# The first two column pairs of each feed-forward stage by plain block products instead of Winograd products

## The chip, the cores and the metric

The kernel runs on one core of one Trainium2 chip. The metric is the device time of one execution in microseconds (us); before the change it is 2248.64 us, the median of 3 runs (2248.58 to 2249.43).

## What is computed

One layer: a feed-forward stage, a mixer of four branches, a second feed-forward stage, over 1024 tokens with 1024 features, in float32. The change touches the two feed-forward stages alone (D = 1024, F = 2816):

```python
def _rmsnorm(x, w):
    y = x * rsqrt(mean(x * x, axis=-1) + EPS)
    return y * w

def _swiglu(x, wg, wu, wd):
    return (silu(x @ wg) * (x @ wu)) @ wd

x = x + 0.5 * _swiglu(_rmsnorm(x, ffn1_norm), ffn1_wg, ffn1_wu, ffn1_wd)
...
x = x + 0.5 * _swiglu(_rmsnorm(x, ffn2_norm), ffn2_wg, ffn2_wu, ffn2_wd)
```

## The kernel before

**Values.** x is held transposed, as 8 blocks of 128 features by 1024 tokens, in tiles of two blocks and 512 tokens (one half of the tokens). Each float32 operand of a product is split into hi and lo (ScalarE, ACT, writes hi; VectorE, DVE, writes lo, in `split` or `left_plain`), and a product of blocks is three matmuls on TensorE (PE): hi·hi, lo·hi, hi·lo (`one`, L1161 to L1163). All matmuls of the stages are 128x128 weights against 128x512 values.

**Gate and up products.** F is cut into 22 columns f of 128; each has a gate and an up part. `gate_up` computes for each f the two 512-token halves of gate and up with Winograd's seven products instead of eight: the left blocks are A11, A12 (tokens' first half, features' first and second half), A22, and the sums S1 to S4 of blocks of x; the right ones are made from the weights of f in `prep_gate` and `prep_up`. A product is 4 blocks of 128 features, so 12 matmuls, and a column is 84. `first` is A11 times gate, `second` adds A12 times gate to the same PSUM tile, `rest` issues S2, S1, S4, A22 and S3 and adds the products on DVE. `act` multiplies by the norm's factor `scale` and applies SiLU; `spill` sends each two columns' sums to DRAM. `down` then multiplies by wd, likewise by Winograd's scheme.

**The norm.** The gain goes into the left blocks, the factor 1/rms (one number for each token) is applied behind the products, in `act`. `square` and `add_squares` make the sum of squares, `mean` (16 tiny matmuls `ms`, L1099) sums over features, `rsqrt` is a chain of 11 small DVE operations that ends in `rs_y` (L157), 8 matmuls `r` (L1117) spread it over the partitions and ACT copies it to `scale` (L1118).

**The start of a stage.** The sums S1 to S4 need all of x and time on DVE. To give PE work in the meantime, `left` opens columns 0 to 3 ahead: `open` issues `first`, `open_second` issues `second`, so 8 products of 12 matmuls; the sums, their splits and the squares are written between them. Then `gate_up` takes the S2 and S1 products of column 0, and `rms` is a background generator that issues `ms` after them and `r` after a pause. In stage 1, x comes from DRAM, the sums of squares are added on DVE; in stage 2, x comes from the mixer's last product (`product`, L260 to L266) and they are added on GpSimd (POOL).

**What sets the order.** PE follows the program's order; ACT, DVE, POOL and SP (which issues the DMAs) follow an order that the scheduler sets when the program is built, each strictly in that order.

Of the kernel before, what the change touches and what calls it, by code (L numbers as in the profile page):

```python
# [976 lines left out]
class Ffn:  # L977
# [9 lines left out]
    def __init__(self, net, n, es):  # L987
        self.net, self.nc, self.n = net, net.nc, n
        pool = lambda name, bufs: es.enter_context(
            net.tc.tile_pool(name=f"{name}{n}", bufs=bufs, reuse_waits="tile")  # L990
        )
# [4 lines left out]
        self.preps, self.raw_gate = {}, {}
        self.gain = net.col(f"ffn{n}_norm")
        self.ms, self.squares = None, {}
        self.opened = {}

# [203 lines left out]
    def act(self, f, g, u):  # L1204
# [22 lines left out]

    def open(self, f):

        self.prep_gate(f)  # L1230
        self.opened[f] = [*self.first(f), None]

    def open_second(self, f):
        self.opened[f][2] = self.second(f, self.opened[f][0])
        if f:
            self.raw_gate.pop(f)

    def gate_up(self, also):

        net = self.net  # L1240
        self.acts = {}
        waiting = []

        def acts():
            net.bg.finish()
            while waiting:
                waiting.pop(0)()

        for f in range(NF):
            self.prep_up(f)  # L1250
            self.prep_gate(f + 1)
            if f in self.opened:
                _, t, g = self.opened.pop(f)
                waiting.append(self.rest(f, t, g, mid=acts))
            else:
                x, t = self.first(f)
                waiting.append(self.rest(f, t, None, x))
            if f:
                acts()
            if f == 2:  # L1260
                also()
# [160 lines left out]
def build(ctx, tc, a, cols):  # L1422
# [15 lines left out]
    def left(ffn, x0, x1, engine, late):  # L1438

        ffn.open(1)  # L1440
        for i in range(2):
            ffn.open_second(i)
        ffn.open(2)
        ffn.left_s2(x0[:2], x1[2:])
        ffn.prep_up(0)
        ffn.open(3)
        for i in (2, 3):
            ffn.open_second(i)
        ffn.left_s1(x1[:2], x1[2:])
        ffn.add_squares(engine)  # L1450
        for q, kp in late:
            ffn.square((x0, x1)[q][kp], q, kp)
            ffn.add_squares(engine)
        ffn.left_rest(x0[:2], x0[2:], x1[2:])
        n.bg.add(ffn.rms(4, 7))

    with ExitStack() as es:
# [20 lines left out]
        for q, xs in ((0, x0), (1, x1)):
            for kp in range(2):
                ffn.square(xs[kp], q, kp)  # L1480
        ffn.left_cross(x0[:2], x1[:2])
        left(ffn, x0, x1, nc.vector, [(q, kp) for q in range(2) for kp in (2, 3)])
# [117 lines left out]
```

## Time and profile before

| | us |
|---|---|
| median of 3 runs | 2248.64 |
| the profiled execution | 2247.78 |
| its span | 2246.0 |
| PE busy | 2191.7 (98%) |
| DVE busy | 1377.5 (61%) |
| ACT busy | 873.0 (39%) |
| chain that ended last: PE | 89% |
| chain that ended last: DVE | 6% |

The profiled execution is one run; its span is from the first to the last instruction, and 1.78 us of its time lie around it. The chain that ended last is followed back from the last instruction: it says which engine the end waited for. PE is busy nearly all the time over the whole span, so a share of the span says little about the start of a stage; what a step there costs is read in the stretch itself.

### The profile page before, as it was taken

How to read it: one execution, taken by the hardware profiler on the slowest of the kernel's cores; microseconds unless marked ns; L12 is line 12 of the kernel's file. 1: busy time of each engine (PE TensorE's matmuls, PEld its weight loads, DVE VectorE, ACT ScalarE, POOL GpSimd, SP SyncE). 2: the span in 40 equal slices, each digit the busy share in tenths (PEclk: the TensorE clock that was granted, in tenths of full speed). 3: DMA queues.
4: the chain of work that ended last, by engine and by line, in shares of the span. 5: the costliest groups of instructions: out<-in, count | busy, mean ns of one | idle time of the engine just before them, and what ended most of it. 6: DMA issues, size and time to landing. Idle time of an engine off the chain costs nothing.

```text
span 2246.0 us, 26117 instructions
## 1 busy us (share of the span) xinstructions
PE 2191.7 (98%) x10144; PEld 1782.3 (79%) x10144; DVE 1377.5 (61%) x1925; ACT 873.0 (39%) x1154; POOL 327.3 (15%) x227
## 2 busy tenths in 40 slices
PE   6899999999999999999999999999889999999999
PEld 5688888888887777788877778888678888888887
DVE  8788787887773446315255233035778777778764
ACT  7223332234443533326477363134423323224332
POOL 0000000000013344322343434411000000000000
PEclk9899999999999999999999999999989999999999
DMA  4233232394333122231111222116223232249432
GB/s 153 82 100 113 91 117 94 129 330 164 105 130 110 52 75 72 82 118 56 59 55 45 81 80 78 53 52 195 67 94 117 94 111 101 98 144 326 150 118 94
DMA packets 115484, 246.15 MB, mean 110 GB/s; under 512 B 11296, under 2 KB 23200, under 8 KB 115360
## 3 DMA queue, kind: packets, MB, share of 16 engines
q1 hardware_dynamic: 115360, 244.48, 32.5%
q8 instruction: 79, 1.29, 0.2%
q14 instruction: 45, 0.37, 0.1%
HBM read 182.05 MB, written 62.39 MB: 109 GB/s over the span
## 4 chain that ended last, share of the span: by engine, by line
PE 89%; DVE 6%; ACT 2%; issue 2%; POOL 1%; DMA 0%; SPq 0%; POOLq 0%; ACTq 0%; DVEq 0%
PE X L1163 3%; PE X L1161 3%; PE X L1162 3%; PE S2p L1163 2%; PE S2p L1161 2%; PE S2p L1162 2%; PE S4p L1161 2%; PE Ad L1345 2%; PE S4p L1163 2%; PE S1p L1161 2%; PE S4p L1162 2%; PE Ad L1344 2%; PE S1p L1162 2%; PE S1p L1163 2%; PE Ad L1343 2%; PE S3p L1161 2%
## 5 line engine op out<-in xcount | busy, mean ns | idle before, releaser
L56 POOL TENSOR_TENSOR wlo<-raw,whi 128x1024 fp32r<-128x1024 f32 x56 | 136.0, 2429 | 249.3 <-ACT whi L55 237.6
L1011 ACT ACTIVATE uhi<-gu 128x1024 fp32r<-128x1024 f32 x44 | 46.8, 1063 | 263.5 <-issue 135.8
L55 ACT ACTIVATE whi<-raw 128x1024 fp32r<-128x1024 f32 x72 | 76.0, 1057 | 184.6 <-PE o L261 22.3
L964 DVE TENSOR_TENSOR gt<-gt,wb 128x512 f32<-128x512 f32 x48 | 32.9, 686 | 135.7 <-PE wb L956 77.5
L1011 ACT ACTIVATE ghi<-gu 128x1024 fp32r<-128x1024 f32 x44 | 46.7, 1061 | 168.0 <-DMA gu<-wgu 154.8
L191 POOL TENSOR_TENSOR nm0lo<-res,nm0hi 128x1024 fp32r<-128x1024 f32 x2 | 5.0, 2484 | 638.2 <-ACT nm0hi L190 638.2
L1011 ACT ACTIVATE ahiS<-inS 128x1024 fp32r<-128x1024 f32 (+1 forms) x48 | 46.9, 989 | 131.3 <-PE Dd L1344 31.7
L1012 DVE TENSOR_TENSOR aloS<-inS,ahiS 128x1024 fp32r<-128x1024 f32 (+1 forms) x48 | 54.5, 1135 | 60.9 <-ACT ahiS L1011 60.9
L1161 PE MATMUL X<-A11hi,ghi 128*128 128x512 f32 x176 | 71.9, 409 | 13.2 <-ACT ghi L1011 13.2
L1208 ACT ACTIVATE a<-a 128x1024 f32<-128x1024 f32 x44 | 46.8, 1063 | 85.6 <-DVE a L1207 85.6
L965 POOL TENSOR_TENSOR m<-m,gt 128x512 f32<-128x512 f32 x48 | 62.2, 1297 | 119.8 <-DVE gt L964 118.1
L1163 PE MATMUL X<-A11hi,glo 128*128 128x512 f32 x176 | 72.4, 412 | 5.5 <-DVE glo L1012 5.5
L1163 PE MATMUL S2p<-S2hi,tlo 128*128 128x512 f32 x176 | 70.6, 401 | 4.0 <-DVE tlo L1012 4.0
L1161 PE MATMUL S2p<-S2hi,thi 128*128 128x512 f32 x176 | 70.2, 399 | 3.8 <-ACT thi L1011 3.8
L1162 PE MATMUL X<-A11lo,ghi 128*128 128x512 f32 x176 | 71.2, 404 | 0.0
L1161 PE MATMUL X<-A12hi,ghi 128*128 128x512 f32 x176 | 68.6, 390 | 2.6 <-ACT t L1171 2.6
L1162 PE MATMUL S2p<-S2lo,thi 128*128 128x512 f32 x176 | 70.1, 399 | 0.0
L1161 PE MATMUL S4p<-S4hi,uhi 128*128 128x512 f32 x176 | 69.4, 394 | 0.0
L1162 PE MATMUL S4p<-S4lo,uhi 128*128 128x512 f32 x176 | 68.7, 391 | 0.0
L1163 PE MATMUL S4p<-S4hi,ulo 128*128 128x512 f32 x176 | 68.7, 390 | 0.0
L1345 PE MATMUL Ad<-ahiA,dloA 128*128 128x512 f32 x176 | 68.7, 390 | 0.0
L1161 PE MATMUL S1p<-S1hi,thi 128*128 128x512 f32 x176 | 68.7, 390 | 0.0
(1209 smaller groups left out, 6774.2 us busy)
## 6 DMA issues: line engine op xcount, KB each, us to landing
gu<-wgu SPq DMA_DIRECT2D x94, 512.0 KB, 3.5
raw<-w_in SPq DMA_DIRECT2D x56, 512.0 KB, 3.5
acts<-s SPq DMA_DIRECT2D x88, 256.0 KB, 2.9
wd<-wd SPq DMA_DIRECT2D x40, 512.0 KB, 6.5
inS<-acts SPq DMA_DIRECT2D x40, 512.0 KB, 3.7
acts<-a SPq DMA_DIRECT2D x66, 256.0 KB, 3.3
inA<-acts SPq DMA_DIRECT2D x30, 512.0 KB, 3.6
res<-x SPq DMA_DIRECT2D x16, 512.0 KB, 6.8
```

The source lines that it names most:

```text
L55: nc.scalar.activation(hi, raw, AF.Copy)
L56: getattr(nc, self.lo_engine[i]).tensor_tensor(lo, raw, hi.bitcast(F32), op=ALU.subtract)
L965: nc.gpsimd.tensor_tensor(m, m, g, op=ALU.add)
L1011: self.nc.scalar.activation(hi, src, AF.Copy)
L1012: self.nc.vector.tensor_tensor(lo, src, hi.bitcast(F32), op=ALU.subtract)
L1161: mm(ps, whi[:, s], hi, start=start and k == 0, stop=False, skip_group_check=True)
L1162: mm(ps, whi[:, s], lo, start=False, stop=False, skip_group_check=True)
L1163: mm(ps, wlo[:, s], hi, start=False, stop=k == 3, skip_group_check=True)
L1208: nc.scalar.activation(g, g, AF.Silu)
L1343: mm(outs[t], whi[:, j, m], ahi[:, j], start=first, stop=False, skip_group_check=True)
L1344: mm(outs[t], whi[:, j, m], alo[:, j], start=False, stop=False, skip_group_check=True)
L1345: mm(outs[t], wlo[:, j, m], ahi[:, j], start=False, stop=last, skip_group_check=True)
```

## The change

In both stages columns 0 and 1 are no longer made by Winograd's seven products, and no column is opened ahead. Instead they are made by eight plain block products: for each f, each half of the tokens q and each of gate and up (j), `half` issues 8 blocks of 128 features, 24 matmuls (L1246 to L1248), into one PSUM tile, and ACT copies it to `early` (L1250). That needs the left blocks A11, A12, A21 and A22 split as they are (A21 is new) and the weights of columns 0 and 1 split as they are (`plain_right`). `early_act` applies scale and SiLU to both columns at the start of `gate_up`, which then takes columns 2 to 21 by the seven products as before. `rms` is no generator any more: `ms` is issued behind the plain products of column 0, `r` (`spread`) behind those of column 1. Each column now ends with its own `act`. The diff, cut:

```diff
-    def left_rest(self, a11, a12, a22):
+    def left_rest(self, a11, a12):
         for kp in range(2):
             self.scaled_with(a12[kp], a12[kp], 4 + 2 * kp, self.s2[kp], ALU.subtract)
         self.left_split("S4", a12)
-        self.left_plain("A22", a22, 4)
         self.left_split("S3", a11)
...
+    def plain_right(self, f, j):
+        tag = "rg" if f == 0 else ("rt", "ru")[j]
+        raw = self.load(2 * f + j)
+        self.plain[f, j] = self.split(raw, *(self.t4(tag, f"p{part}{f}{j}", F32R) for part in ("hi", "lo")))
+
+    def half(self, f, q):
+        mm = self.nc.tensor.matmul
+        names = (("A11", "A12"), ("A21", "A22"))[q]
+        for j in range(2):
+            whi, wlo = self.plain[f, j]
+            ps = self.net.ps(f"h{f}{q}{j}")
+            for k in range(NK):
+                s = slice(k % 4 * P, (k % 4 + 1) * P)
+                hi, lo = (t[:, k % 2] for t in self.xc[names[k // 4]][k % 4 // 2])
+                mm(ps, whi[:, k // 4, s], hi, start=k == 0, stop=False, skip_group_check=True)
+                mm(ps, whi[:, k // 4, s], lo, start=False, stop=False, skip_group_check=True)
+                mm(ps, wlo[:, k // 4, s], hi, start=False, stop=k == NK - 1, skip_group_check=True)
+            self.early[f, q, j] = t = self.t2("ts"[q], f"e{f}{q}{j}")
+            self.nc.scalar.copy(t, ps)
+
+    def early_act(self, f):
+        nc = self.nc
+        V = nc.vector
+        a = self.t4("a", f"a{f}")
+        for q in range(2):
+            g, u = (self.early[f, q, j] for j in range(2))
+            V.tensor_tensor(g, g, self.scale[:, q], op=ALU.mult)
+            nc.scalar.activation(g, g, AF.Silu)
+            V.tensor_tensor(u, u, self.scale[:, q], op=ALU.mult)
+            V.tensor_tensor(a[:, q], g, u, op=ALU.mult)
+        self.put(f, a)
...
-        for f in range(NF):
+        for f in range(2):
+            self.early_act(f)
+        for f in range(2, NF):
             self.prep_up(f)
             self.prep_gate(f + 1)
...
     def left(ffn, x0, x1, engine, late):
-        ffn.open(1)
-        for i in range(2):
-            ffn.open_second(i)
-        ffn.open(2)
-        ffn.left_s2(x0[:2], x1[2:])
-        ffn.prep_up(0)
-        ffn.open(3)
-        for i in (2, 3):
-            ffn.open_second(i)
-        ffn.left_s1(x1[:2], x1[2:])
-        ffn.add_squares(engine)
-        for q, kp in late:
+        for j in range(2):
+            ffn.plain_right(1, j)
+        ffn.half(0, 0)
+        for q, kp in late[:4]:
             ffn.square((x0, x1)[q][kp], q, kp)
             ffn.add_squares(engine)
-        ffn.left_rest(x0[:2], x0[2:], x1[2:])
-        n.bg.add(ffn.rms(4, 7))
+        ffn.left_plain("A21", x1[:2], 0)
+        ffn.left_plain("A22", x1[2:], 4)
+        ffn.half(1, 0)
+        for q, kp in late[4:]:
+            ffn.square((x0, x1)[q][kp], q, kp)
+            ffn.add_squares(engine)
+        ffn.half(0, 1)
+        ffn.rms()
+        ffn.left_cross(x0[:2], x1[:2])
+        ffn.left_s2(x0[:2], x1[2:])
+        ffn.half(1, 1)
+        ffn.prep_gate(2)
+        ffn.prep_up(2)
+        ffn.spread()
+        ffn.left_s1(x1[:2], x1[2:])
+        ffn.left_rest(x0[:2], x0[2:])
```

Three places, as the engines' orders show them. ACT at the start of stage 1, before the change (t is the copy of `first`'s PSUM tile X, ghi the hi part of a column's gate weights, sq a square):

```order
L1171 COPY t0_1_149<-X0_136 128x512
L1011 ACTIVATE ghi1_1_157<-gu2_1_155 128x1024
L1080 ACTIVATE sq00_1_183<-n0x0_1_114 128x1024
L1080 ACTIVATE sq01_1_185<-n0x1_1_122 128x1024
L1080 ACTIVATE sq10_1_187<-n1x0_1_175 128x1024
```

and the same place after it (e is the copy of a plain product's PSUM tile h, phi the hi part of a plain column's weights):

```order
L1079 ACTIVATE sq00_1_234<-n0x0_1_114 128x1024
L1079 ACTIVATE sq01_1_236<-n0x1_1_122 128x1024
L1079 ACTIVATE sq02_1_239<-n0x2_1_136 128x1024
L1079 ACTIVATE sq03_1_242<-n0x3_1_138 128x1024
L1250 COPY e001_1_232<-h001_207 128x512
L1029 ACTIVATE A21hi1_1_247<-n1x1_1_162,c_small_76 128x512
L1011 ACTIVATE phi10_1_170<-gu2_1_168 128x1024
```

The split of the third set of weights, phi10, now stands behind the copy of the second plain product h001 and one half of A21.

DVE at the end of the norm's chain in stage 1, before the change (tlo is the lo part of column 1's weights for S2 and S1):

```order
L1147 TENSOR_TENSOR tt1_1_528<-gu3_1_525,tt1_1_528 128x512
L155 TENSOR_TENSOR f1rs_t_454<-f1rs_y_453 128x8
L1150 TENSOR_TENSOR gu2_1_523<-gu2_1_523,tt1_1_528 128x512
L156 SCALAR_TENSOR_TENSOR f1rs_t_454<-f1rs_t_454,v1_451 128x8
L157 SCALAR_TENSOR_TENSOR f1rs_y_453<-f1rs_t_454,f1rs_y_453 128x8
L155 TENSOR_TENSOR f1rs_t_454<-f1rs_y_453 128x8
L1012 TENSOR_TENSOR tlo1_1_532<-tt1_1_528,thi1_1_531 128x1024
L156 SCALAR_TENSOR_TENSOR f1rs_t_454<-f1rs_t_454,v1_451 128x8
L157 SCALAR_TENSOR_TENSOR f1rs_y_453<-f1rs_t_454,f1rs_y_453 128x8
L155 TENSOR_TENSOR f1rs_t_454<-f1rs_y_453 128x8
L156 SCALAR_TENSOR_TENSOR f1rs_t_454<-f1rs_t_454,v1_451 128x8
L157 SCALAR_TENSOR_TENSOR f1rs_y_453<-f1rs_t_454,f1rs_y_453 128x8
```

and after it (S1lo and S3lo are lo parts of left sums, gu7 the up weights of column 3):

```order
L1012 TENSOR_TENSOR glo3_1_604<-gu6_1_601,ghi3_1_603 128x1024
L155 TENSOR_TENSOR f1rs_t_408<-f1rs_y_407 128x8
L1012 TENSOR_TENSOR tlo2_1_507<-tt2_1_503,thi2_1_506 128x1024
L156 SCALAR_TENSOR_TENSOR f1rs_t_408<-f1rs_t_408,v1_405 128x8
L1012 TENSOR_TENSOR S1lo0_1_541<-n1x0_1_160,S1hi0_1_540 128x1024
L157 SCALAR_TENSOR_TENSOR f1rs_y_407<-f1rs_t_408,f1rs_y_407 128x8
L1012 TENSOR_TENSOR S1lo1_1_543<-n1x1_1_162,S1hi1_1_542 128x1024
L155 TENSOR_TENSOR f1rs_t_408<-f1rs_y_407 128x8
L1144 TENSOR_TENSOR gu7_1_713<-gu7_1_713 128x512
L156 SCALAR_TENSOR_TENSOR f1rs_t_408<-f1rs_t_408,v1_405 128x8
L1012 TENSOR_TENSOR S3lo1_1_563<-n0x1_1_122,S3hi1_1_562 128x1024
L157 SCALAR_TENSOR_TENSOR f1rs_y_407<-f1rs_t_408,f1rs_y_407 128x8
```

Between v, which reads `ms`, and the last L157 stood 11 small operations, 4 of 128x512 and one split; now there are 11 small ones, 2 `scalar_tensor_tensor` and 1 `tensor_tensor` of 128x512, and 8 splits.

DVE behind `r` in stage 1, after the change, the last 12 rows up to column 3's tlo (the ten before them, from the first row of L1258 on, are of `early_act` too):

```order
L1260 TENSOR_TENSOR e111_1_492<-e111_1_492,scale_1_519 128x512
L1190 TENSOR_TENSOR t2_1_620<-S2p2_622,t2_1_620 128x512
L1261 TENSOR_TENSOR a1_1_577<-e110_1_465,e111_1_492 128x512
L1147 TENSOR_TENSOR tt3_1_716<-gu7_1_713,tt3_1_716 128x512
L1223 TENSOR_TENSOR s1_0_1_586<-a0_1_568,a1_1_577 128x512
L1150 TENSOR_TENSOR gu6_1_601<-gu6_1_601,tt3_1_716 128x512
L1224 TENSOR_TENSOR s2_0_1_587<-s1_0_1_586,a0_1_568 128x512
L1012 TENSOR_TENSOR glo4_1_735<-gu8_1_732,ghi4_1_734 128x1024
L1225 TENSOR_TENSOR s4_0_1_589<-a1_1_577,s2_0_1_587 128x512
L1226 TENSOR_TENSOR s3_0_1_588<-a0_1_568 128x512
L1194 TENSOR_TENSOR w2_1_650<-S1p2_651,t2_1_620 128x512
L1012 TENSOR_TENSOR tlo3_1_720<-tt3_1_716,thi3_1_719 128x1024
```

The work of `early_act` and of one `spill` now stands ahead of column 3's tlo; before, the work of `act` for columns held back, with their `spill`, stood there.

## Rows read from the trace of the kernel before

**Rows 1.** The page, busy time of the engines: us, share of the span, instructions.
```profile
PE 2191.7 (98%) x10144; PEld 1782.3 (79%) x10144; DVE 1377.5 (61%) x1925; ACT 873.0 (39%) x1154; POOL 327.3 (15%) x227
```

**Rows 2.** Waits of PE in stage 1: us in total, times, longest.
```profile
PE r L1117 <- DVE f1rs_y L157: 10.4, 1, 10.4
...
PE S2p L1163 <- DVE tlo L1012: 2.2, 1, 2.2
PE S2p L1161 <- ACT thi L1011: 1.9, 1, 1.9
```

**Rows 3.** PE in order of time, stage 1: start, us, then [idle before <-releaser].
```profile
7.60 0.79 PE L1161 MATMUL X<-A11hi,ghi 128*128 128x512 f32 x1 [7.60 <-ACT ghi L1011]
...
9.21 0.79 PE L1163 MATMUL X<-A11hi,glo 128*128 128x512 f32 x1 [0.39 <-DVE glo L1012]
...
48.33 3.63 PE L1099 MATMUL ms<-mean_col,sq 128*128 128x1 f32 x32
62.37 3.78 PE L1117 MATMUL r<-c_ident,f1rs_y 128*128 128x128 f32 x16 [10.41 <-DVE f1rs_y L157]
...
101.85 0.39 PE L1163 MATMUL S3p<-S3hi,ulo 128*128 128x512 f32 x1
...
112.12 0.39 PE L1163 MATMUL S1p<-S1hi,tlo 128*128 128x512 f32 x1
...
465.27 0.39 PE L1343 MATMUL Ad<-ahiA,dhiA 128*128 128x512 f32 x1
```

**Rows 4.** The same view, stage 2.
```profile
1583.21 0.39 PE L1161 MATMUL X<-A11hi,ghi 128*128 128x512 f32 x1
...
1630.22 3.78 PE L1117 MATMUL r<-c_ident,f2rs_y 128*128 128x128 f32 x16 [4.61 <-DVE f2rs_y L157]
...
1669.18 0.39 PE L1163 MATMUL S3p<-S3hi,ulo 128*128 128x512 f32 x1
...
1679.18 0.39 PE L1163 MATMUL S1p<-S1hi,tlo 128*128 128x512 f32 x1
...
2032.35 0.39 PE L1343 MATMUL Ad<-ahiA,dhiA 128*128 128x512 f32 x1
```

**Rows 5.** The same view, stage 1, first and last of 24 matmuls without a wait.
```profile
42.89 0.39 PE L1161 MATMUL S2p<-S2hi,thi 128*128 128x512 f32 x1
...
48.10 0.39 PE L1163 MATMUL S1p<-S1hi,tlo 128*128 128x512 f32 x1
```

**Rows 6.** Stretches: us, busy (count) of PE, PEld, DVE, ACT, POOL, granted clock, DMA.
```profile
7.60:62.30 54.70, 37.99 (x152) 29.41 (x152) 52.28 (x91) 38.20 (x50) 0.00 (x0) 0.86 0.35 122
...
16.40:19.80 3.40, 3.40 (x8) 2.72 (x9) 3.11 (x11) 2.88 (x4) 0.00 (x0) 0.51 0.89 336
...
1623.90:1625.60 1.70, 1.70 (x9) 1.63 (x9) 0.00 (x0) 0.30 (x1) 0.00 (x0) 0.52 0.00 0
```

**Rows 7.** ACT in order of time, stage 1.
```profile
9.13 2.65 ACT L1029 ACTIVATE A12hi<-n0x,c_small 128x512 fp32r<-128x512 f32 x4
13.50 0.59 ACT L1171 COPY t<-X 128x512 f32<-128x512 f32 x1 [1.72 <-PE X L1163]
13.98 1.06 ACT L1011 ACTIVATE ghi<-gu 128x1024 fp32r<-128x1024 f32 x1
...
64.47 0.59 ACT L1118 COPY scale<-r 128x512 f32<-128x512 f32 x1 [3.78 <-PE r L1117]
```

**Rows 8.** DVE in order of time, stage 1, up to v, the start of the norm's chain.
```profile
55.15 1.21 DVE L1012 TENSOR_TENSOR S3lo<-n0x,S3hi 128x1024 fp32r<-128x1024 f32 x1
56.28 0.68 DVE L1194 TENSOR_TENSOR w<-S1p,t 128x512 f32<-128x512 f32 x1
56.88 0.15 DVE L1109 TENSOR_SCALAR v<-ms 128x8 f32<-128x8 f32 x1
```

**Rows 9.** Stage 2: POOL in order of time; DVE by line, ns min/median/max.
```profile
1585.42 5.21 POOL L1088 TENSOR_TENSOR sq<-sq,sq 128x1024 f32<-128x1024 f32 x2 [18.43 <-ACT sq L1080]
...
L1044 DVE SCALAR_TENSOR_TENSOR S<-o1x,c_small,o0x x4: 737/1813/2901, 1585.5 to 1591.8; 128x512 f32<-128x512 f32 x4
```

More of the change, by code (lines that the diff above doesn't have):

```diff
@@ L998, in __init__ @@
         self.ms, self.squares = None, {}
-        self.opened = {}
+        self.plain, self.early, self.acts = {}, {}, {}
     def t4(self, tag, name, dtype=F32):
@@ L1015, in xc_tiles @@
     def xc_tiles(self, name):
-        tag = {"A11": "h0", "A12": "h0", "S2": "h1", "S1": "h1"}.get(name, "xc")
+        tag = {"A11": "h0", "A12": "h0", "S2": "h1", "S1": "h1", "A21": "h1"}.get(name, "xc")
         return [[self.t4(tag, f"{name}{part}{kp}", F32R) for part in ("hi", "lo")] for kp in range(2)]
@@ L1101, in mean, with rms @@
                 )
-    def rms(self, first, pause):
+    def rms(self):
         nc, net = self.nc, self.net
-        yield first
         for q in range(2):
@@ L1178, in second, with rest @@
         return g
-    def rest(self, f, t, g, x=None, mid=lambda: None):
+    def rest(self, f, t, g, x=None):
         nc, net = self.nc, self.net
@@ L1210, in act, with put @@
         V.tensor_tensor(g, g, u, op=ALU.mult)
-        self.acts[f] = g
+        self.put(f, g)
+    def put(self, f, a):
+        self.acts[f] = a
         if f % 2:
@@ L1226, in spill @@
             nc.sync.dma_start(self.net.a["acts"][self.NAMES.index(name), c], t)
[L1228 to L1236, printed above, removed]
-    def gate_up(self, also):
[L1240 to L1247, printed above, removed]
-        for f in range(NF):
+    def plain_right(self, f, j):
+        tag = "rg" if f == 0 else ("rt", "ru")[j]
+        raw = self.load(2 * f + j)
+        self.plain[f, j] = self.split(raw, *(self.t4(tag, f"p{part}{f}{j}", F32R) for part in ("hi", "lo")))
@@ L1250, in gate_up @@
             self.prep_up(f)
             self.prep_gate(f + 1)
[L1252 to L1260, printed above, removed]
+            x, t = self.first(f)
+            self.rest(f, t, None, x)()
+            if f == 3:
                 also()
@@ L1468, in build @@
         x0 = [load(0, 0)]
-        ffn.prep_gate(0)
+        ffn.plain_right(0, 0)
         x0.append(load(0, 1))
         ffn.left_plain("A11", x0, 0)
-        ffn.open(0)
         x0 += [load(0, k) for k in (2, 3)]
-        ffn.prep_gate(1)
         ffn.left_plain("A12", x0[2:], 4)
+        ffn.plain_right(0, 1)
         n.ident = n.const("ident")
         x1 = [load(1, k) for k in range(4)]
[L1478 to L1482, printed above, removed]
+        left(ffn, x0, x1, nc.vector, [(q, kp) for q in range(2) for kp in range(4)])
         ffn.gate_up(n.derive)
@@ L1501, in build @@
                     ffn.left_plain(("A11", "A12")[c], x[q][2 * c : 2 * c + 2], 4 * c)
-                elif c == 0:
-                    ffn.left_cross(x[0][:2], x[1][:2])
-        ffn.open(0)
+        for j in range(2):
+            ffn.plain_right(0, j)
         left(ffn, x[0], x[1], nc.gpsimd, [])
```

8 lines of the change are left out of this document (4 added, 4 removed).

## The prediction, made before the changed kernel had run

> **What bounds the kernel now.** I read the page first: PE is busy 2191.7 us of the 2246.0 us span [rows 1], so a gain must come from PE's idle time, from its slow-clock time or from fewer matmuls. The change gives it more matmuls. The waits of PE, asked for stage 1 up to the first matmul of `down`, then show where the idle time lies [rows 2]: the longest, 10.4 us, is `r` waiting for the norm's chain on DVE; 2.2 and 1.9 us are one column's S2 waiting for its split weights. PE in order of time puts them in place [rows 3]: first matmul at 7.60, `ms` at 48.33, `r` at 62.37, the S2 waits between 101.85 and 112.12, `down` at 465.27. Stage 2 has the same shape [rows 4]: start 1583.21, `r` 1630.22, S2 waits between 1669.18 and 1679.18, `down` 2032.35. The stretches say what DVE does up to `r` in stage 1: 52.28 of 54.70 us busy [rows 6]. So DVE, not PE, sets the time of `r` there, and PE idles behind it.
>
> That gives the cut that I use: from a stage's start to `r`, and from `r` to `down`. What lies outside the two stages is the same code; I give it no change.
>
> **Prices.** A matmul at full clock: 24 of them start from 42.89 to 48.10, so 23 steps in 5.21 us, 0.227 us each [rows 5]. At the half clock (1.2 instead of 2.4 GHz): 8 matmuls in 3.40 us at granted 0.51 [rows 6], 0.425 each, where 15 would have gone; such a stretch costs 7 x 0.227 = 1.6 us. DVE: a split of 128x1024 takes 1.13 (55.15 to 56.28), a `tensor_tensor` of 128x512 0.60 (56.28 to 56.88) [rows 8].
>
> **From r to down.** Before, 120 matmuls of a stage stand ahead of `r` (8 products of the opened columns, S2 and S1 of column 0), so 22 x 84 - 120 = 1728 stand behind it. Now 2 x 96 = 192 stand ahead and 20 x 84 = 1680 behind. Behind `r` that is 48 fewer: -10.9 us in each stage, although a stage has 24 matmuls more. They are moved to where PE waited.
>
> The S2 waits belong to column 3, the fourth: its weights' split stood on DVE behind the `act` work of the columns held back. From 101.85 to 112.12 15 steps took 10.27 instead of 3.40: 6.9 us, slow clock included [rows 3]; in stage 2 10.00, so 6.6 us [rows 4]. Do they go? In stage 1, `r` will start at about 63.5 (below); the first `scale` is ready 2.7 us behind it (64.47 + 0.59 against 62.37 [rows 3, 7]), at 66.2. From there to tlo of column 3, DVE has 22 operations: 2 splits at 1.13 and 20 of 128x512 at 0.60, 14.3 us. With 2 us for `scale`'s second half and the SiLU it waits for (an estimate: 64.47's copy is followed by another, 0.59 each, and each SiLU is of that size), tlo is ready at 82.5. PE wants it after `r` (3.8), column 2 (84) and 14 of column 3: 63.5 + 3.8 + 98 x 0.227 = 89.5. So 7 us are to spare, and I take both waits as gone: -6.9 and -6.6. Bounds: 0 kept, or all kept.
>
> After the wait, `r` runs at the half clock before and mostly will again. In stage 1 I allow +1.0 for a slow stretch behind it (between 0, as slow as now, and 1.6), in stage 2, where PE will hardly wait, +0.8.
>
> **From the start to r, stage 1.** Two things have to be ready.
> PE: 7.6 until the weights are there, 0.4 waiting for their lo part as now (0.39 at 9.21 [rows 3]), 2.0 since the first ten matmuls run slow, 144 x 0.227 = 32.7 for the three plain groups ahead of `ms`. In between one new wait: the third set of weights, phi10, stands on ACT behind the copy of the second plain product and half of A21. The nearest row is the second column's start now: copy 0.59, split 1.06 [rows 7], to which comes 2.65 / 4 = 0.66: 2.3 us, 0.5 for the lo part, and one slow stretch, 1.6. Then `ms`, 3.6. Sum: 50.7. The last 48 matmuls, 10.9, bring PE to `r` at 61.6.
> DVE: total work up to rs_y hardly changes. Both orders have 15 splits of 128x1024; 4 `left_plain` operations of about 0.7 for A21 come in, 5 of 0.60 (three weight sums, two product sums) move behind. Now the chain ends just ahead of `r` at 62.37 [rows 3]; by work alone it would end at 62. But behind v, which needs `ms` at 50.7, stand 8 splits (9.0), two of 0.74, one of 0.60 and 11 small ones, some 0.1 each beyond the work they stand between: 12.3. So rs_y not before 63.0, `r` at 63.5: 1.1 later than now, with a wait of 2 instead of 10.4. Bounds: 62.4 (nothing later), and 72 if DVE idled behind `ms` as long as PE does now.
>
> **From the start to r, stage 2.** Now 47.0 us [rows 4]. PE: 192 x 0.227 = 43.6, `ms` 3.6: 47.2. DVE has only 3 larger operations between the 11 small ones there, about 5.5 us, beside 48 matmuls of 10.9: hidden, and no wait is left. During `ms` the granted clock fell, to 0.52 from 1623.9 on [rows 6]; it may do so again with matmuls behind it, so between 0 and 1.6: I take 0.8. Then +1.0.
> The two POOL additions of squares fall beside DVE's splits of A22. Beside them a 128x512 operation of DVE grew from 0.74 to 2.90 us [rows 9], two of them, 4.3 us in all. The A22 parts are wanted 96 matmuls, 21.8 us, after the start, and DVE idles in between: I take 0.
> The Trainium skill (GPSIMD Engine Reference, Key points) says that GpSimd shares its SBUF interfaces with VectorE and contends with its instructions that have two SBUF inputs. By that the plain weights' splits can be hit as well, and the sum would be up to about 2 us worse.
>
> **The sum.** Stage 1: -10.9 - 6.9 + 1.0 + 1.1 = -15.7. Stage 2: -10.9 - 6.6 + 0.8 + 1.0 = -15.7. Together -31.4: the profiled execution's 2247.8 becomes 2216.4. The median of the runs lies 0.9 above the profiled execution, so I say 2217.
> Other edits: six loads of 512 KB fewer, since opened columns loaded their gate weights twice; no row of PE's waits names a load [rows 2, 3], so nothing. More work on ACT (A21, eight copies): it has 38.20 busy of 54.70 [rows 6], and only the wait counted above. Two columns fewer of product sums on DVE, in place of `early_act`: counted up to tlo.
>
> **Rivals.**
> (a) The S2 waits stay. Of DVE's waits behind `r` I counted 2 us; if ACT's SiLUs hold it longer, column 3 waits as now: 13.5 us less gain, 2231. Against it: the 7 us to spare. It decides when tlo of column 3 is later than that.
> (b) `r` comes late in stage 1, since DVE waits for ACT's hi parts in turn, one behind the other. For it: DVE's total there is as large as now and ACT's larger. At the upper bound, 72 instead of 63.5: 2225.
> (c) The slower one: in the plain block each matmul needs another part from ACT or DVE, PE halts shortly again and again, and the clock stays at half through it: 192 x 0.2 = 38 us in stage 1 alone, 2255. It decides at some 160 slow matmuls of a block. Against it: the opened columns now wait for their parts in the same way, and the stretch up to `r`, with `r`'s long wait in it, still has 0.86 granted [rows 6]. The Trainium skill (TensorE: Matmul & The Clock Gate, A second HAM failure mode) tells of such a kernel, whose frequent short idles kept the clock swinging; no row here shows it in a stretch without a long wait.
> (d) Nothing moves, since the scheduler would set DVE's order so that `r` is as much later as PE gained. Against it: the order shows `r` behind about the same work. 2246.
>
> **Chances.** Forecast, with its bounds 2210 to 2222: 0.74. (a) 0.10, (b) 0.09, (c) 0.04, (d) 0.03. About 0.2%, 4.5 us, is what a measurement of this kernel tells from no change. Forecast, (a) and (b) are faster beyond it: 0.93; (d) is the same: 0.03; (c) slower: 0.04. Without the slow stretches and with `r` no later in either stage it is 2217 - 1.0 - 0.8 - 1.0 - 1.1 = 2213; the low end, 2208, leaves as much again for prices that rest on single rows. The high end, 2228, takes in (b) and most of the way to (a).
>
> **What would show it.** In the new profile `r` of stage 1 starts at 62 to 65 behind a wait of 1 to 3 us; in stage 2 about 48 us behind its start, with no wait; PE waits once for the third set of weights, 2 to 3 us; no S2 wait on thi or tlo; from `r` to `down` about 385 us in both stages instead of 402.9 and 402.1. It is wrong if PE's granted clock is near 0.5 through the plain block, or if PE waits for tlo or glo behind `r`.

## The result: 2211.9 us, 1.7% faster

The median of the changed kernel is 2211.91 us (2211.23 to 2215.67, 4 runs), that of the kernel before beside it 2249.03; the ratio is 0.9833, with a 95% interval of 0.9821 to 0.9846. The profiled execution took 2211.46 us, with a span of 2209.7. The page, busy time of the engines, answers to [rows 1]:

```profile
PE 2186.5 (99%) x10192; PEld 1782.2 (81%) x10192; DVE 1352.3 (61%) x1897; ACT 876.8 (40%) x1166; POOL 328.6 (15%) x227
```

PE has 48 matmuls more and is busy 5.2 us less: busy time counts a matmul at half clock for longer. The waits of PE in stage 1, against [rows 2]:

```profile
PE h L1246 <- ACT phi L1011: 10.1, 2, 7.8
PE r L1117 <- DVE f1rs_y L157: 1.4, 1, 1.4
PE h L1248 <- DVE plo L1012: 1.3, 2, 0.9
```

The 7.8 is the start itself. No S2 waits any more, and in stage 2 the view has no line at all. PE in order of time, stage 1, against [rows 3] (h is a plain product, X the first product of column 2):

```profile
7.78 0.80 PE L1246 MATMUL h<-A11hi,phi 128*128 128x512 f32 x1 [7.78 <-ACT phi L1011]
...
24.31 0.50 PE L1246 MATMUL h<-A11hi,phi 128*128 128x512 f32 x1 [2.30 <-ACT phi L1011]
...
47.40 3.63 PE L1098 MATMUL ms<-mean_col,sq 128*128 128x1 f32 x32
...
65.10 2.05 PE L1117 MATMUL r<-c_ident,f1rs_y 128*128 128x128 f32 x16 [1.43 <-DVE f1rs_y L157]
66.90 0.48 PE L1161 MATMUL X<-A11hi,ghi 128*128 128x512 f32 x1
...
89.24 0.39 PE L1163 MATMUL S2p<-S2hi,tlo 128*128 128x512 f32 x1
...
447.82 0.39 PE L1356 MATMUL Ad<-ahiA,dhiA 128*128 128x512 f32 x1
```

and stage 2, against [rows 4]:

```profile
1566.20 0.39 PE L1246 MATMUL h<-A11hi,phi 128*128 128x512 f32 x1
...
1598.84 3.63 PE L1098 MATMUL ms<-mean_col,sq 128*128 128x1 f32 x32
1602.33 0.49 PE L1246 MATMUL h<-A21hi,phi 128*128 128x512 f32 x1
...
1613.35 1.95 PE L1117 MATMUL r<-c_ident,f2rs_y 128*128 128x128 f32 x16
...
1615.06 0.48 PE L1161 MATMUL X<-A11hi,ghi 128*128 128x512 f32 x1
...
1995.97 0.39 PE L1356 MATMUL Ad<-ahiA,dhiA 128*128 128x512 f32 x1
```

From the first matmul to `down`, stage 1 takes 440.04 us instead of 457.67 [rows 3], stage 2 429.77 instead of 449.14 [rows 4]: -17.6 and -19.4. What lies outside them adds 0.7, and that makes the 36.3 us between the spans.

A yardstick for what follows is a stage's length if PE ran at full clock and never waited: its matmuls at 5.21 / 23 = 0.2265 us [rows 5], 3.5 for `ms` and 1.7 for `r` (both from stage 2 above). That is 1848 x 0.2265 + 5.2 = 423.8 for the kernel before and 1872 x 0.2265 + 5.2 = 429.2 now. Before, the stages stood 33.9 and 25.3 us above it; now 10.8 and 0.6. The change pays 5.4 us more of matmuls in each stage and gets 23.1 and 24.7 us of waits and slow clock for it.

### The profile page after: what moved, and what is told of

The parts are those of the page before. It is cut to its first block, busy times and chain, and to the rows that moved or that the text cites. A ratio compares the mean times of both kernels' runs of the same rounds, so it can differ in the third digit from the quotient of the medians.

```text
span 2209.7 us, 26198 instructions
## 1 busy us (share of the span) xinstructions
PE 2186.5 (99%) x10192; PEld 1782.2 (81%) x10192; DVE 1352.3 (61%) x1897; ACT 876.8 (40%) x1166; POOL 328.6 (15%) x227
## 4 chain that ended last, share of the span: by engine, by line
PE 91%; DVE 4%; ACT 2%; issue 2%; POOL 1%; DMA 0%; SPq 0%; POOLq 0%; ACTq 0%; DVEq 0%
PE X L1163 3%; PE X L1162 3%; PE X L1161 3%; PE Ad L1358 2%; PE Ad L1356 2%; PE Ad L1357 2%; PE S2p L1163 2%; PE S3p L1163 2%; PE A22p L1163 2%; PE S4p L1163 2%; PE S1p L1163 2%; PE S3p L1162 2%; PE A22p L1162 2%; PE S4p L1162 2%; PE S1p L1162 2%; PE S2p L1162 2%
## 5 line engine op out<-in xcount | busy, mean ns | idle before, releaser
L1011 ACT ACTIVATE ahiA<-inA 128x1024 fp32r<-128x1024 f32 (+1 forms) x36 | 35.4, 988 | 85.5 <-PE Ad L1357 31.3
L1356 PE MATMUL Ad<-ahiA,dhiA 128*128 128x512 f32 x176 | 68.5, 389 | 0.0
L1357 PE MATMUL Ad<-aloA,dhiA 128*128 128x512 f32 x176 | 68.5, 389 | 0.0
L1199 DVE TENSOR_TENSOR a<-S3p,a 128x512 f32<-128x512 f32 x40 | 27.7, 691 | 61.2 <-PE S3p L1163 61.2
L1012 DVE TENSOR_TENSOR vlo<-gu,vhi 128x512 fp32r<-128x512 f32 x40 | 27.7, 692 | 60.3 <-PE A22p L1162 57.9
L1161 PE MATMUL X<-A11hi,ghi 128*128 128x512 f32 x160 | 62.4, 390 | 0.0
L1163 PE MATMUL X<-A11hi,glo 128*128 128x512 f32 x160 | 62.3, 389 | 0.0
L1162 PE MATMUL X<-A11lo,ghi 128*128 128x512 f32 x160 | 62.2, 389 | 0.0
L1161 PE MATMUL S2p<-S2hi,thi 128*128 128x512 f32 x160 | 62.2, 389 | 0.0
L1163 PE MATMUL S2p<-S2hi,tlo 128*128 128x512 f32 x160 | 62.2, 389 | 0.0
```

Of the source, the lines that this page charges most:

```text
L1011: self.nc.scalar.activation(hi, src, AF.Copy)
L1012: self.nc.vector.tensor_tensor(lo, src, hi.bitcast(F32), op=ALU.subtract)
L1161: mm(ps, whi[:, s], hi, start=start and k == 0, stop=False, skip_group_check=True)
L1162: mm(ps, whi[:, s], lo, start=False, stop=False, skip_group_check=True)
L1163: mm(ps, wlo[:, s], hi, start=False, stop=k == 3, skip_group_check=True)
L1356: mm(outs[t], whi[:, j, m], ahi[:, j], start=first, stop=False, skip_group_check=True)
```

## Experiments

| kernel | edit | median, us | ratio to before, 95% | stage 1 | stage 2 |
|---|---|---|---|---|---|
| before | | 2249.03 | | 457.7 | 449.1 |
| the change | | 2211.91 | 0.9833 (0.9821 to 0.9846) | 440.0 | 429.8 |
| e1 | before, weights ahead of act | 2241.33 | 0.9962 (0.9950 to 0.9975) | 455.9 | 445.5 |
| e9 | before, `r` 48 matmuls later | 2242.92 | 0.9968 (0.9956 to 0.9979) | 457.2 | 443.2 |
| e10 | e9 and e1 | 2241.01 | 0.9952 (0.9939 to 0.9965) | 454.1 | 443.7 |
| e11 | e9, weights behind S1 | 2238.81 | 0.9951 (0.9936 to 0.9965) | 456.5 | 438.2 |
| e6 | one plain column, stage 1 | 2228.03 | 0.9902 (0.9889 to 0.9916) | 451.0 | 432.9 |
| e12 | e6, weights behind S1 | 2220.62 | 0.9871 (0.9855 to 0.9888) | 447.3 | 429.8 |
| e2 | `r` 12 matmuls later | 2214.26 | 0.9836 (0.9822 to 0.9849) | 439.0 | 432.9 |
| e3 | loads ahead, stage 1 | 2215.33 | 0.9841 (0.9828 to 0.9855) | 441.6 | 429.8 |
| e4 | one plain column, stage 2 | 2212.70 | 0.9830 (0.9816 to 0.9843) | 441.2 | 430.2 |
| e5 | `ms` spread | 2212.67 | 0.9833 (0.9820 to 0.9847) | 441.4 | 429.9 |
| e7 | e3, weights behind S1 | 2207.94 | 0.9815 (0.9802 to 0.9828) | 435.2 | 431.4 |
| e8 | e7, e4 and e5 in one | 2202.17 | 0.9784 (0.9771 to 0.9798) | 432.4 | 427.2 |

Each ratio is to the kernel before timed beside it. The stages are those of the profiled executions, from PE in order of time, first matmul to the first of `down`.

### Would another order of the old products do?

The prediction said that 48 matmuls move ahead of `r` into PE's wait, and that column 3's S2 waits go since its tlo no longer stands behind `act`. Each can be had without a plain product. e1 takes the second alone:

```diff
                 waiting.append(self.rest(f, t, None, x))
+            if f in (1, 2):
+                self.prep_up(f + 1)
             if f:
                 acts()
```

> The kernel before, with one thing changed in gate_up: in columns 1 and 2 the next column's weights are prepared (prep_up) ahead of their own act. Nothing up to r changes. Theory A, that of the prediction (the S2 waits of column 3 come from DVE's order, in which act work stands ahead of tlo of column 3): tlo3 comes about 3.5 us earlier in stage 1 (105.78 to about 102.3, since two operations of 1.13 us of act and one split of 1.13 us no longer stand ahead), PE wants it at about 103, so most of the 6.9 and 6.6 us goes: 2249 becomes 2236 to 2242. Rival B (DVE is behind because opened columns leave PE only 60 matmuls, 13.6 us, for a column of DVE work; order does not matter): the wait moves to a later product, and the time stays within 2 us of 2249.

Measured: 2241.33, inside A's range, but with less than half of what A counted on. The wait for thi of column 3 is gone in both stages, that for tlo is still there in both (the waits of PE in stage 1 of e1):

```profile
PE S2p L1163 <- DVE tlo L1012: 2.2, 1, 2.2
```

From `r` to `down` 2.2 us less in stage 1 (400.7), 3.6 in stage 2 (398.5). Order is part of the cause, 5.8 of the 13.5 us.

e9 takes the first alone:

```diff
-                waiting.append(self.rest(f, t, g, mid=acts))
+                waiting.append(self.rest(f, t, g, mid=acts if f else lambda: None))
```

> The kernel before, with one thing changed: the acts that column 0's rest calls no longer finish the norm's generator, so that r stands behind column 0's S4, A22 and S3 and column 1's S2 (48 matmuls, 10.9 us, as many as the change moves ahead of r), and ms 6 matmuls later. No plain product, no matmul more. Theory A (any matmuls ahead of r fill PE's wait; plain columns are only one way): r starts at 63 to 66 us with a wait of 0 to 3 instead of 10.4, in stage 2 with none instead of 4.6, and the S2 waits stay at about what they are or shrink, since DVE's own idle 10 us behind r (62.3 to 75) go too: 2230 to 2237. Rival B (DVE is short of time up to column 3, so what is won at r is lost again at the S2 waits): these grow by 5 us or more in stage 1, and the time stays within 5 us of 2250.

Measured: 2242.92, outside both ranges; stage 2 gained 6.0 us as A says, stage 1 0.5, as B says. PE in order of time, stage 1 of e9:

```profile
69.82 0.80 PE L1161 MATMUL S2p<-S2hi,thi 128*128 128x512 f32 x1 [5.11 <-ACT thi L1011]
...
75.52 2.30 PE L1117 MATMUL r<-c_ident,f1rs_y 128*128 128x128 f32 x16
...
104.25 0.50 PE L1161 MATMUL S2p<-S2hi,thi 128*128 128x512 f32 x1 [1.92 <-ACT thi L1011]
...
107.15 0.80 PE L1163 MATMUL S2p<-S2hi,tlo 128*128 128x512 f32 x1 [2.17 <-DVE tlo L1012]
```

`r` has no wait, but column 1's S2 now waits 5.1 us for its weights, and column 3's S2 starts at 104.25, where it started before the edit at 104.15 (PE in order of time, the kernel before):

```profile
104.15 0.50 PE L1161 MATMUL S2p<-S2hi,thi 128*128 128x512 f32 x1 [1.92 <-ACT thi L1011]
```

So 48 matmuls ahead of `r`, with nothing else changed, are worth next to nothing in stage 1. e10 puts e1's edit on top:

> As e9, and with the preparation of the next column's weights ahead of act in columns 1 and 2, as in e1. Theory A (order is all that the kernel before lacked): both parts add up, 10.9 + 4.6 for r and the 2.2 + 3.6 that e1 gave: 2225 to 2232, still above the changed kernel, since opened columns give PE 60 matmuls for a column of DVE work. If order alone were enough, with no PE wait left, it would be 2 x 5.4 us below the changed kernel's stages at full clock, about 2201 (48 matmuls fewer in all). Rival B (DVE's shortage): 2238 or more.

2241.01: B. e11 prepares the weights of columns 1 to 3 earlier still, behind the S1 product of the column before:

```diff
+        def mid(f):
+            if f:
+                acts()
+            if f < 3:
+                self.prep_up(f + 1)
...
-                waiting.append(self.rest(f, t, g, mid=acts))
+                waiting.append(self.rest(f, t, g, mid=lambda: mid(f)))
```

> As e9 (the kernel before with r behind column 1's S2), and with the weights of columns 1, 2 and 3 prepared behind the S1 product of the column before them, so ahead of its last sums and its act on DVE: the order that took the S2 waits out of the plain kernel in e7. Theory A (the plain columns pay since they ask less of DVE for each matmul; an order can move the shortage but not end it): the waits for thi of 5.1 us in column 1 and 1.9 + 2.2 us in column 3 shrink in stage 1 but others stay or come up (lo parts of S4, tlo, glo, r); stage 1 stays above 450, the time 2228 to 2240. Rival B (order is all): no wait for thi, tlo or r behind 50 us in stage 1; what is left is its start, and stage 1 falls to about 442 or less, stage 2 to 436 or less, the time to 2215 to 2225, or below the changed kernel.

2238.81, stage 1 456.5: A. The waits of PE in stage 1 of e11:

```profile
PE X L1161 <- ACT ghi L1011: 11.4, 3, 7.8
PE r L1117 <- DVE f1rs_y L157: 3.9, 1, 3.9
PE X L1163 <- DVE glo L1012: 3.4, 4, 1.6
PE S2p L1163 <- DVE tlo L1012: 3.3, 2, 2.0
PE S2p L1161 <- ACT thi L1011: 1.9, 1, 1.9
```

The same five kinds of wait as in the kernel before, whose view has 11.1, 10.4, 2.9, 2.2 and 1.9 for them: that for `r` lost 6.5 us, three of the others grew by 1.9 together, and two smaller ones came in (0.8 and 0.5). That is 3.3 us of waits less, yet stage 1 is only 1.2 us shorter: the other 2 us went to the clock, which was at half near 31, 55, 65 and 123 us. In stage 2, where DVE was busy 38.70 of the 47.0 us up to `r` and not 52.28 of 54.7 as in stage 1 [rows 6], the order of e11 was worth 11.0 of the 25.3 us above the yardstick. No order tried here brought stage 1 of the old products below 454.

### What the plain columns change

The stretches up to the end of column 3's tlo, first the kernel before, then the changed one (us, busy and count of PE, PEld, DVE, ACT, POOL, granted clock, DMA):

```profile
7.60:107.00 99.40, 78.60 (x326) 62.94 (x326) 85.05 (x134) 51.20 (x64) 0.00 (x0) 0.89 0.31 107
```

```profile
7.78:81.30 73.52, 68.52 (x303) 55.79 (x304) 67.49 (x115) 50.08 (x67) 0.00 (x0) 0.98 0.35 124
```

DVE has 17.6 us less to do until that point, beside 303 matmuls instead of 326. Some 4.7 us of this are order and not amount: four of column 2's product sums and two operations of its `act` (4 x 0.60 + 2 x 1.13 by [rows 8]) stand ahead of that tlo in the kernel before and behind it in the changed one. By [rows 8] a plain column costs DVE 2 splits of 1.13 and 6 operations of 0.60, 5.9 us, and gives PE 96 matmuls, 21.8 us. A Winograd column costs 6 of 1.13 (three splits, three of `act`) and 11 of 0.60 (four weight sums, one split, six product sums), 13.4 us, for 84 matmuls, 19.1 us; opened ahead, it gives PE 60 of them, 13.6 us, behind `r`, for 12.3 us of DVE. Whether DVE's amount alone holds stage 1 of e11, or also the single pair of u weights and the wait for `scale`, was not separated: DVE idled there too, 4.5 us for `scale` among it.

e6 takes one plain column of stage 1 back:

```diff
-        left(ffn, x0, x1, nc.vector, [(q, kp) for q in range(2) for kp in range(4)])
+        left_one(ffn, x0, x1)
```

(the second line reads so in place of the first; `left_one` issues `half(0, 0)` and `half(0, 1)`, then `ms`; column 1 goes by the seven products, and `r` stands behind its S1.)

> The changed kernel, with only column 0 plain in stage 1 (144 matmuls ahead of r: 96 plain ones and four products of column 1, instead of 192); stage 2 is unchanged. Theory A (in stage 1 DVE's work up to rs_y sets when r starts, and the plain columns only fill PE's time until then): r stays at 62 to 66 us, PE waits some 11 us more ahead of it, and 36 more matmuls stand behind it (1716 instead of 1680): stage 1 grows by about 8.2 us, 2220. Rival B (PE's own order sets r: with ms 11 us earlier, v and rs_y come earlier too): r starts at 52 to 58 us, and stage 1 grows by less than 2 us or gets shorter by up to 2.7 us, 2209 to 2214.

Measured: 2228.03. PE in order of time, stage 1 of e6:

```profile
56.18 1.95 PE L1117 MATMUL r<-c_ident,f1rs_y 128*128 128x128 f32 x16
...
76.06 0.80 PE L1161 MATMUL S2p<-S2hi,thi 128*128 128x512 f32 x1 [6.19 <-ACT thi L1011]
```

The loss came, 11.0 us in stage 1, but not at `r`: that moved to 56.18 without a wait, where rival B had it, and the time was lost at the next column's S2. A's reason was wrong: DVE's work ahead of `r` is not fixed, the scheduler puts more or less of it there; what is due is the work up to the next weights. (7 us more lie in the mixer, whose program is the same; in this execution the clock was at half there for 17.0 us, in that of the change for 3.4.) e12 puts that preparation ahead, behind column 1's S1:

```diff
     def late(self):
+        self.prep_up(2)
         self.spread()
         self.early_act(0)
```

> As e6 (one plain column in stage 1), with the weights of column 2 prepared behind column 1's S1 product, so ahead of r's copies, the early act and column 1's act on DVE, as e7 did it for two plain columns. Theory A (in stage 1 the second plain column buys DVE time that no order gives): the wait of 7.4 us at column 2's S2 shrinks to 0 to 4 us, but what stands behind it on DVE is late in its turn; stage 1 stays longer than the 440.0 of the changed kernel, 2214 to 2224. Rival B (e6 lost its time to that one place in DVE's order): no wait behind r in stage 1, which then is the changed kernel's or shorter, down to 437.3 (12 matmuls fewer): 2209 to 2212.

2220.62: A. The wait moved on to column 3's S2, the waits of PE in stage 1 of e12:

```profile
PE S2p L1161 <- ACT thi L1011: 2.6, 1, 2.6
PE X L1163 <- DVE glo L1012: 2.0, 1, 2.0
...
PE S2p L1163 <- DVE tlo L1012: 1.1, 1, 1.1
```

So the second plain column of stage 1 is worth 7.3 us against the better of the two orders tried without it, although it is 12 matmuls, 2.7 us, longer; against e7 below, the best order found with it, it is 12.1 us.

### What is left in the changed kernel

e2 moves `spread` and the early acts behind column 2's first product:

```diff
             x, t = self.first(f)
+            if f == 2:
+                self.spread()
+                for e in range(2):
+                    self.early_act(e)
```

> The changed kernel, with r and the early_act work issued behind the first product of column 2 (12 matmuls, 2.7 us) instead of ahead of it, in both stages. Theory A (in stage 1 PE comes to r 1.4 us too early, DVE's chain sets it; behind r PE has work without a gap): the wait of 1.43 goes, nothing else changes: about 2210.5, stage 1 1.4 us shorter, stage 2 the same. Rival B (r sets when column 3's tlo comes, and 2.7 us more of delay brings the S2 wait back): tlo3 is ready 8 us ahead of PE now, so it would take much more; if it does come back, 2213 or more.

Measured: 2214.26. Stage 1 got 1.0 us shorter, `r` without a wait, as A says; stage 2, where nothing but `r`'s place differs, got 3.2 longer, and that not at `r`:

```profile
1598.95 4.14 PE L1098 MATMUL ms<-mean_col,sq 128*128 128x1 f32 x32
1602.96 0.77 PE L1246 MATMUL h<-A21hi,phi 128*128 128x512 f32 x1
```

(PE in order of time, stage 2 of e2.) The clock fell while `ms` ran, 4.01 us instead of 3.49, and 13 matmuls behind it took 0.43 each: 0.5 + 2.6.

e4 takes one plain column out of stage 2, by the `left_one` of e6 without its squares:

```diff
-        left(ffn, x[0], x[1], nc.gpsimd, [])
+        left_one(ffn, x[0], x[1])
```

> The changed kernel, with only column 0 plain in stage 2 (96 instead of 192 matmuls ahead of ms or between ms and r); column 1 goes by the seven products, and r stands behind its first four products, 48 matmuls behind ms as now. Stage 1 is unchanged. Theory A (in stage 2 PE has no wait and the second plain column is only 12 matmuls too many): 12 x 0.227 = 2.7 us less, 2209. Rival B (without the second plain column the sums and their splits are late, since DVE needs the time up to 1615 for S1, S3 and the weights): PE waits for lo parts of S2, S1, S4 or S3 in column 1, in all 3 us or more, and the time is 2212 to 2220.

Measured: 2212.70, no wait of PE in stage 2 (B is out), and yet nothing gained. Two stretches of stage 2 of e4, around `ms` and behind it:

```profile
1588.80:1592.40 3.60, 3.60 (x29) 3.60 (x27) 3.60 (x5) 2.92 (x5) 0.00 (x0) 0.80 0.02 5
1592.40:1606.40 14.00, 14.00 (x54) 11.56 (x54) 10.66 (x23) 6.71 (x9) 0.00 (x0) 0.81 0.12 37
```

`ms` and 12 matmuls took 9.5 us instead of 6.2: the 2.7 were won and 3.3 lost to the clock. e5 spreads `ms` between plain products (`half`, behind every second block of column 0's second token half):

```diff
+                if (f, q) == (0, 1) and k % 2:
+                    self.mean(j, k // 2)
```

> The changed kernel, with the 16 matmuls of ms no longer in one block but two behind every second 128-feature block of the last plain product pair of column 0 (the 48 matmuls ahead of it), in both stages; nothing else. Theory A (the granted clock falls because PE does nothing but these tiny matmuls for 3.6 us): no stretch at half clock behind ms in either stage, so stage 1 is 1.6 us shorter than the 440.0 of the changed kernel and stage 2 stays at 430.0: about 2210. Rival B (the clock falls for the waits ahead, or each tiny matmul costs more between large ones): a half-clock stretch near 50 us stays, or the 48 + 16 matmuls take over 14.5 us at full clock: 2212 or more.

Measured: 2212.67. No half clock is left behind `ms` in stage 1, and none came in stage 2, where the profile of the change had none either; in stage 1, 42 matmuls with the 16 small ones among them take 13.19 us, 0.227 each. That speaks for A on the clock, and e8 below does so again. The time is no better, since in this execution the clock was at half behind the wait for the third set of weights (27 to 31 us): the 24 matmuls there took 9.1 us from first start to the next product, in the profile of the change 6.8. In e2 and e4, whose programs are the same up to there, they took 8.4 and 9.1. Stretches of e5, that one and those with `ms`:

```profile
27.00:31.00 4.00, 4.00 (x11) 3.13 (x10) 4.00 (x6) 4.00 (x7) 0.00 (x0) 0.50 0.79 212
36.90:52.00 15.10, 15.10 (x83) 12.90 (x81) 14.03 (x19) 8.62 (x13) 0.00 (x0) 1.00 0.00 0
1588.00:1604.00 16.00, 16.00 (x88) 13.71 (x87) 4.98 (x7) 5.84 (x8) 0.00 (x0) 1.00 0.11 34
```

e3 aims at that wait:

```diff
         ffn.plain_right(0, 1)
+        for j in range(2):
+            ffn.plain_right(1, j)
         n.ident = n.const("ident")
         x1 = [load(1, k) for k in range(4)]
```

> The changed kernel, with the weights of column 1 loaded (and split, in program order) ahead of the second half of x in stage 1; stage 2 has the same program with its plain weights in one loop. Theory A (ACT's order holds PE for 2.30 + 0.88 us at the third set of weights; DVE then only waits for ms): both waits go, ms comes up to 3.2 us earlier, v by up to 2.7, since DVE waits 2.67 us for ms now, and r by 2 to 2.7 us: 2209 to 2210. Rival B (DVE's total work up to rs_y sets r whatever PE does): PE's waits of 3.2 us turn into a longer wait at r, 1.4 becomes 4 to 4.6 us, and the time stays at 2212.

Measured: 2215.33, and neither theory had it. `r` came at 58.98 without a wait, 6 us earlier; then the S2 waits of column 3 came back, here with the order of DVE ahead of them (the waits of PE, then DVE in order of time):

```profile
PE S2p L1161 <- ACT thi L1011: 2.7, 1, 2.7
PE S2p L1163 <- DVE tlo L1012: 1.8, 1, 1.8
```

```profile
81.28 1.22 DVE L1206 TENSOR_TENSOR a<-a,scale 128x1024 f32<-128x1024 f32 x1
82.42 1.22 DVE L1208 TENSOR_TENSOR u<-u,scale 128x1024 f32<-128x1024 f32 x1
83.55 0.68 DVE L1147 TENSOR_TENSOR tt<-gu,tt 128x512 f32<-128x512 f32 x1
84.33 1.23 DVE L1209 TENSOR_TENSOR a<-a,u 128x1024 f32<-128x1024 f32 x1
85.47 1.22 DVE L1012 TENSOR_TENSOR ulo<-gu,uhi 128x1024 fp32r<-128x1024 f32 x1
86.61 1.22 DVE L1012 TENSOR_TENSOR tlo<-tt,thi 128x1024 fp32r<-128x1024 f32 x1
```

Column 2's `act` stands ahead of column 3's sum tt. e7 prepares column 3's weights behind column 2's S1:

```diff
-            self.rest(f, t, None, x)()
+            self.rest(f, t, None, x, (lambda: self.prep_up(3)) if f == 2 else lambda: None)()
```

> The kernel of the loads ahead (e3) with one thing more: the weights of column 3 are prepared behind column 2's S1 product in the program, so ahead of column 2's act on DVE. Theory A (in e3 the S2 waits of column 3, 2.66 + 1.77 us, come from DVE's order, with column 2's act and two splits ahead of tlo): both waits and the half-clock stretch behind them (2.5 us) go, r stays at 59: stage 1 becomes about 434.7 long instead of 441.6, and the time about 2206. Rival B (DVE is short of time there whatever the order): the waits move to a product of column 3 or 4, and the time stays at 2210 to 2215.

2207.94, stage 1 435.2: A. All waits of PE that are left in stage 1 of e7 lie at its start:

```profile
PE h L1247 <- ACT phi L1011: 7.6, 1, 7.6
PE h L1249 <- DVE plo L1012: 0.4, 1, 0.4
```

With two plain columns order is enough; with opened columns (e9 to e11) or one plain one (e12) the orders tried were not.

### All in one

e8 has the edits of e7 (the loads of stage 1 alone), e4 and e5.

> All in one: the loads of stage 1 ahead, column 3's weights prepared ahead of column 2's act, ms between the plain products, and one plain column only in stage 2. If the parts add up: stage 1 433 to 435 long, stage 2 430.0 - 2.7 = 427.3 (the 4.3 us of matmuls lost to the half clock in e4 gone), 2200 to 2204. If they don't, e4's and e3's waits or half-clock stretches come back in another place: 2206 or more.

e8 took 2202.17 us: stage 1 432.4, stage 2 427.2. Its interval lies below that of the change. (The text on record puts e4's loss to the clock at 4.3; it is 3.3.) Its stretches from the start of stage 1 to `r`, and from `r` to `down`:

```profile
7.75:57.50 49.75, 49.36 (x224) 40.76 (x225) 45.01 (x85) 37.82 (x51) 0.00 (x0) 1.00 0.36 136
57.50:440.10 382.60, 382.60 (x1697) 317.08 (x1697) 310.20 (x391) 121.03 (x149) 0.00 (x0) 1.00 0.34 118
```

PE is busy without a gap but for 0.39 us. Stage 1 is 3.2 us above its yardstick of 429.2, its first matmuls at half clock among it, stage 2 0.7 above 1860 x 0.2265 + 5.2 = 426.5: what is left in the stages is matmuls.

## Why the prediction was right, and where it was off

The forecast was 2217 (2208 to 2228), the result 2211.9: sign, range and most of the mechanism held, the size was 5 us short.

**From r to down** was to fall by 16.8 us in stage 1 (10.9 + 6.9 - 1.0) and 16.7 in stage 2 (10.9 + 6.6 - 0.8). It fell by 20.2 (402.90 to 382.72) and 19.5 (402.13 to 382.62). The S2 waits are gone, as forecast: tlo of column 3 was ready at 81.3 (82.5 said) and wanted at 89.24 (89.5 said). That both times came out so close is luck: `r` was 1.6 us late, but the first `scale` was ready 1.8 us behind it and not 2.7, DVE then ran up to tlo without the 2 us of waits that were allowed, and `r` took 1.8 us of PE and not 3.8.

**The mis-sized term is the clock at r**: "After the wait, `r` runs at the half clock before and mostly will again", with +1.0 and +0.8 behind it. `r` ran at full clock, 1.8 and 1.7 us to the next matmul instead of 3.4 in both stages before ([rows 3, 4] and these two rows of the kernel before, the matmuls behind `r`):

```profile
65.80 0.77 PE L1161 MATMUL S4p<-S4hi,uhi 128*128 128x512 f32 x1
...
1633.66 0.73 PE L1161 MATMUL S4p<-S4hi,uhi 128*128 128x512 f32 x1
```

No slow stretch followed, and the one that had lain behind `r` before, at a cost of 0.8 and 0.3 us, is gone too. The prediction's lower bound, "as slow as now", left no room for a faster `r`, although it had taken away most of the wait in front of it (1.4 us instead of 10.4 in stage 1, none instead of 4.6 in stage 2). In stage 1 that is 1.0 + 1.6 + 0.8 = 3.4 us more than said, in stage 2 0.8 + 1.7 + 0.3 = 2.8. With 1.4 too little for the start of stage 1, 0.9 too much for that of stage 2 and 0.7 outside, it makes the 5 us.

**From the start to r, stage 1**: 55.9 said, 57.3 measured, with a wait of 1.43 (2 said). The new wait for the third set of weights was sized rightly, 2.30 (2.3 said), behind these rows of ACT in order of time:

```profile
22.13 0.56 ACT L1250 COPY e<-h 128x512 f32<-128x512 f32 x1
22.59 0.72 ACT L1029 ACTIVATE A21hi<-n1x,c_small 128x512 fp32r<-128x512 f32 x1
23.22 1.04 ACT L1011 ACTIVATE phi<-gu 128x1024 fp32r<-128x1024 f32 x1
```

The slow stretch of 1.6 us came not behind this wait but behind `ms` (granted 0.51 from 51.0 to 54.4), so that this term is right by chance: in e2, e4 and e5 the clock did fall behind the wait. rs_y was ready at 65.0, 2 us later than by the sum: the split tlo of column 2, which stands in the norm's stretch, waited 1.58 us for ACT's thi, and thi 3.31 us for the buffer of column 1's plain weights, which PE still read. So PE itself, through ACT and DVE, had a part in when `r` came.

**From the start to r, stage 2**: +0.1 and not +1.0; no wait, as said, and the clock did not fall at `ms`.

**POOL's additions** were to cost 4.3 us on DVE and nothing on PE. The four operations of A22lo took 6.89 us, where four of A22lo take 2.73 in stage 1; they were done at 1576.0 and wanted at 1588 at the earliest: hidden. DVE by line, stage 2 (ns min/median/max):

```profile
L1030 DVE SCALAR_TENSOR_TENSOR A22lo<-o1x,c_small,A22hi x4: 739/1751/2882, 1569.1 to 1575.2; 128x512 fp32r<-128x512 f32 x4
```

Of the plain weights' splits only the last lay beside POOL, for half a microsecond, and took 1.22 us like the others. The up to 2 us that the Trainium skill's rule (GPSIMD Engine Reference, Key points) could have added did not come; the rule itself is borne out by the row above.

**The reason given was half of it.** "They are moved to where PE waited": e9 moved as many and gained 0.5 us in stage 1, since the next wait took over. As far as the runs part them, the gain is of two things together, matmuls ahead of `r` that ask little of DVE, and a DVE that is in time behind `r` too, since it has less to do and a better order to do it in. The count of DVE's operations up to tlo had that, the sentence on `r` did not. And "DVE, not PE, sets the time of `r`" holds for the order that the scheduler set: in e3, e6, e7, e8 and e12 `r` came at 56 to 60.

**The rivals.** (a) did not come, but e3 shows how near it was: an `act` ahead of the sum of column 3's weights brought 4.4 us of S2 waits back. (b) `r` at 65.1, not 72. (c) the plain block ran at a granted 0.97 from the start to `r` by the stretches, which give 1.00 also for the first matmuls, although they start 0.43 us apart as at half clock; what the Trainium skill tells of frequent short idles (TensorE: Matmul & The Clock Gate, A second HAM failure mode) was not met here. (d) is out: 36.3 us moved.

## What to carry to other kernels

Work that fills one engine's wait must be priced on the engine that it waits for: a plain column costs PE 2.7 us more than a Winograd one and the second still won 7 us in stage 1. By the counts above it asks less than half as much of DVE, which fits the gain; no run tried DVE's amount alone. A wait that is removed by order alone can come back at the next place where the late engine's work is due (stage 1 of e3, e9 and e11; in e7 and in stage 2 of e9 it did not), so look for the next due time before counting the gain. Then compare each stage with its matmuls at full clock: it says how much is left (10.8 and 0.6 us here) and when to stop.

## What the runs showed of the hardware that was not expected

The 16 matmuls of `ms` with one column each keep PE busy for 3.5 us, and the granted clock often falls behind or within them, though PE never idles: in the change and e2, e3, e4, e6, e7 and e12, 12 such blocks have no other wait close behind them, and in 8 of these the clock fell, at a price of 1.6 to 3.3 us each, and in 4 it did not; the same matmuls up to there gave both (stage 2 of the change and of e2). Stage 2 of e9, e10 and e11 adds three blocks, two with a fall and one without. Spread among 128x512 matmuls, as in e5 and e8, none of 4 fell, and each small matmul cost about as much as a large one, 0.23 us. The wait of 2.3 us for the third set of weights is as uncertain: behind it the clock fell in e2, e4 and e5 and not in the change, with the same program up to there. Such chance is of the size of the differences between the medians of the change, e2, e4 and e5, which therefore say nothing by themselves; the stages of the traces do.
